# Output product of a hybrid backbone: 512 columns per product in four banks, gate rows fetched through DRAM, and tiles moved to other addresses modulo 128

## The chip, the cores and the metric

The kernel runs on one core of one Trainium2 chip, as one launch. The metric is the device time of that launch in microseconds, the median of several runs. TensorE (PE) multiplies, VectorE (DVE) and ScalarE (ACT) do elementwise work, GpSimd (POOL) does little here, and SyncE (SP) and ScalarE issue the DMA transfers.

## What is computed

A backbone of two layers over 1024 latent tokens and 256 context tokens, model width 1024, all float32. Each layer normalizes and modulates its input, projects it to 3840 columns, runs three branches (window attention, Conformer convolution, bidirectional gated recurrence, each 512 wide), and merges them:

```python
def merge_branches(h, ys, gs, w_branch, w_gate, b_gate, w_out):
    y = jnp.stack([yb.astype(h.dtype) * jax.nn.silu(gb) for yb, gb in zip(ys, gs)], axis=-2)
    proj = jnp.einsum('btnw,nwd->btnd', y, w_branch)
    g = jax.nn.sigmoid(h @ w_gate + b_gate).reshape(h.shape[:-1] + (N_BRANCH, D_MODEL))
    return jnp.sum(proj * g, axis=-2) @ w_out
...
        out = merge_branches(h, (y_att, y_conv, y_lru), (g_att, g_conv, g_lru),
                             w_branch[l], w_gate[l], b_gate[l], w_out[l])
        x_new = deepnorm_post(x, gate[:, None] * out, ln_g[l], ln_b[l])
```

The last product, `@ w_out`, is here called the output product; its result is scaled by `gate`, one value per output column, added to the residual and normalized. The context tokens take the same path in the first layer; in the last layer only what the latents read of them is computed.

## The kernel before

**Precision.** Every float32 operand of a large product is split into a high and a low float32r part (`whi`/`wlo` for weights, `hlhi`/`hllo` and `hchi`/`hclo` for latent and context activations, `yh`/`yl` for branch outputs). Each product is three matmuls, high by high, high by low, low by high, accumulated in one bank of PSUM. In the profile's rows a matmul stands as output <- moving operand, stationary operand, then the sizes of the stationary and the moving tile; each matmul has a weight load of its own (PEld).

**Phases.** Each layer has two phases. Phase 1 computes projections, branches and gate activations, in products whose moving operand is an activation tile of 512 latent tokens or 256 context tokens, and writes gate activations (`th_d`) and branch outputs (`y_d`) to DRAM. Phase 2 (`phase2`) runs over token groups: two groups of 512 latents, and in the first layer then one of 256 context tokens. For each group it does

- the branch products: 3 branches, 8 column chunks of 128, 4 blocks of 128 rows, 3 matmuls: 288 matmuls, moving `yh`/`yl` of 512 tokens, stationary the weights. DVE multiplies each result with a gate activation (`th`, a DMA of 256 KB for each chunk) and sums the three branches into `m`; ACT and DVE split the sum into `mg` (named `hlhi`, `hllo` in the rows, since it lies in the same buffers);
- `gate_rows`: the gate values, which lie along the partitions, are spread over rows of a 128 x 1024 tile `gt`: 8 float32 matmuls against the identity (16 records in the trace) and two copies from PSUM. This is done once for each set of gate values: for the latents in each layer, for the context in the first;
- the output product: for each quarter `qd` of the 1024 output columns (256 columns), for each tile `t` of 128 tokens, 24 matmuls with `mg` stationary and the weights moving, 256 columns each, into one bank; then two DVE operations on 256 columns (`tt` = product times gate row, `xp` = residual times alpha plus `tt`), and the first half of the statistics after the second quarter;
- in a second generator, `norm`: both layer norms of each finished token tile, and in the first layer transposes back (PE, 8 for each tile), modulation and splitting for the next layer.

**Order.** Work is cut into generators that a hand-written planner (`Driver`) interleaves by modelled costs, and the framework's scheduler then fixes each engine's order. Engines and DMA queues run their instructions in that order. Weights come in units of 512 KB (`Wt`): a DMA into `raw` (2 buffers), a copy to `whi` on ACT (4 buffers), a subtraction to `wlo` on DVE (4 buffers). `wfetch(2)` keeps two units ahead of the one in use.

**PSUM.** `psum()` gives one bank of 4 (tag `mm`), `psum2()` two banks together of 2 pairs. Phase 2 uses only `psum()`, for its products and for `norm`'s transposes.

**Addresses.** Tiles lie in SBUF at addresses that follow from the order in which pools are opened, from the left end and from the right end, and from the sizes of tiles (in bytes per partition). The first pool of constants begins at 4096 (scratch) + 128; the constants take 6688, the weights 40960, the activations `hT` 81920, the small tiles 2528. From these, the start addresses modulo 128:

| tiles | layer 0 | layer 1 |
|---|---|---|
| weights `whi`, `wlo`, `raw` | 32 | 32 |
| activations `hlhi`, `hllo`, `hchi`, `hclo`, and `mg` | 32 | 32 |
| branch outputs `yh`, `yl` in phase 2 | 0 | 96 |
| half tiles of phase 1 (`ph`, `qh`, gate weights `lwh`) | 96 | 0 |
| slots of 1328 floats (`vs`, `ks`, `xh`, `P`) | 0 and 64 in turn | 96 and 32 in turn |
| `csr` (4 columns for each of 8 blocks), `ident` | 0 | 0 |

All steps inside the large tiles are multiples of 128 bytes, so that a tile's start gives the residue of each of its blocks.

## Time and profile before

| | |
|---|---|
| median of 3 runs | 2345.81 us (2345.65 to 2347.58) |
| profiled execution, its own time | 2346.24 us |
| its span, first to last instruction | 2344.5 us |
| mean granted clock of TensorE | 0.992 of 2.4 GHz |

One execution is profiled, and rows come from it. A row of a group gives count, busy time, mean duration and the idle time before it. Matmuls overlap in the rows: the duration of one is longer than the step from its start to the next one's start, and the step is what a matmul costs when PE is never idle. Steps are therefore read from the starts in the timeline, over a run of matmuls without gaps.

### The profile page before, as it was taken

The page shows a single profiled execution, that of the slowest core. Times are in us where ns is not written, and L with a number is a line of the kernel's source. Part 1 is how long each engine was busy: PE and PEld are TensorE (multiplying, and loading weights), DVE is VectorE, ACT ScalarE, POOL GpSimd, SP SyncE. Part 2 cuts the span into 40 slices and gives each one's busy share as a digit, 9 for nine tenths or more (in the row PEclk, how much of TensorE's full clock was granted, in tenths as well). Part 3 has the DMA queues.
Part 4 walks back from the last instruction along what each step waited for, and adds up shares of the span by engine and source line. Part 5 has one row for each costly group of instructions (what it writes and reads, how often), then busy time and mean ns, then how long its engine had stood idle before and what let it go on. Part 6 is the DMA issues. An engine that isn't in the chain of part 4 may idle for free.

```text
span 2344.5 us, 32215 instructions
## 1 busy us (share of the span) xinstructions
PE 2280.8 (97%) x12253; PEld 1925.5 (82%) x12253; DVE 1750.5 (75%) x2588; ACT 1066.3 (45%) x1702; POOL 91.2 (4%) x136
## 2 busy tenths in 40 slices
PE   7999999999999999999998899999999999999998
PEld 3888888888888887888888878888888878778988
DVE  5679867869859875448888839979778887657776
ACT  4555553244444565323344535665344456543231
POOL 1000000000000111000101000000000011000000
PEclk8999999999999999999999999999999999999999
DMA  7222323433344332566565622223423334348482
GB/s 279 68 74 97 117 77 124 133 119 103 100 125 125 95 95 91 181 218 217 170 219 166 194 70 65 74 90 128 140 92 95 94 113 135 108 139 276 138 272 72
DMA packets 305819, 309.91 MB, mean 132 GB/s; under 512 B 20608, under 2 KB 239616, under 8 KB 305664
## 3 DMA queue, kind: packets, MB, share of 16 engines
q1 hardware_dynamic: 277152, 255.94, 34.5%
q10 hardware_dynamic: 28512, 51.92, 6.2%
q8 instruction: 96, 1.57, 0.3%
q14 instruction: 59, 0.48, 0.1%
HBM read 232.92 MB, written 74.87 MB: 131 GB/s over the span
## 4 chain that ended last, share of the span: by engine, by line
PE 88%; DVE 5%; ACT 3%; DMA 2%; issue 2%; SPq 0%; POOLq 0%; POOL 0%; ACTq 0%; DVEq 0%
PE ps L73 81%; PE yp L73 3%; PE pt L73 2%; PE pa L73 1%; DVE wlo L73 1%; DMA qd<-qd 1%; ACT whi L73 1%; DVE acc L73 1%; DVE P L73 1%; DVE pl L73 1%; DMA thl<-th 1%; DVE xp L73 0%; DMA raw<-in_w_ada_dram 0%; PE p L73 0%; ACT ph L73 0%
## 5 line engine op out<-in xcount | busy, mean ns | idle before, releaser
L73 PE MATMUL ps<-hlhi,whi 128*128 128x512 f32 x1728 | 683.1, 396 | 2.3 <-DVE gs L73 1.0
L73 PE MATMUL ps<-hllo,whi 128*128 128x512 f32 x1728 | 679.3, 393 | 0.0
L73 PE MATMUL ps<-hlhi,wlo 128*128 128x512 f32 x1728 | 677.7, 393 | 1.1 <-DVE wlo L73 1.1
L73 ACT ACTIVATE whi<-raw 128x1024 fp32r<-128x1024 f32 x240 | 253.8, 1058 | 440.6 <-PE ps L73 406.7
L73 DVE TENSOR_TENSOR wlo<-raw,whi 128x1024 fp32r<-128x1024 f32 x240 | 294.2, 1226 | 124.0 <-ACT whi L73 122.9
L73 PEld LDWEIGHTS ps<-hlhi,wlo 128*128 128x128 f32 x1728 | 325.7, 188 | 70.6 <-DVE wlo L73 2.0
L73 PEld LDWEIGHTS ps<-hlhi,whi 128*128 128x128 f32 x1728 | 326.3, 189 | 68.3 <-DVE pl L73 2.4
L73 PEld LDWEIGHTS ps<-hllo,whi 128*128 128x128 f32 x1728 | 326.1, 189 | 63.6 <-issue 0.7
L73 DVE SCALAR_TENSOR_TENSOR acc<-u,cwt,acc 128x1296 f32<-128x1296 f32 (+1 forms) x240 | 343.0, 1429 | 2.1
L73 PE MATMUL ps<-yh,whi 128*128 128x512 f32 (+1 forms) x480 | 178.0, 377 | 9.3 <-DVE thl L73 6.6
L73 PE MATMUL ps<-yl,whi 128*128 128x512 f32 (+1 forms) x480 | 178.2, 373 | 2.3 <-DVE yl L73 2.3
L73 PE MATMUL ps<-yh,wlo 128*128 128x512 f32 (+1 forms) x480 | 178.9, 374 | 0.0
L73 ACT ACTIVATE ph<-pt 128x512 fp32r<-128x512 f32 x160 | 93.8, 591 | 130.0 <-PE pt L73 124.5
L73 DVE TENSOR_TENSOR pl<-pt,ph 128x512 fp32r<-128x512 f32 x160 | 109.3, 687 | 50.7 <-ACT ph L73 49.3
L73 PE MATMUL ps<-whi,hlhi 128*128 128x256 f32 x512 | 144.3, 284 | 0.0
L73 PE MATMUL ps<-wlo,hlhi 128*128 128x256 f32 x512 | 144.0, 283 | 0.0
L73 PE MATMUL ps<-whi,hllo 128*128 128x256 f32 x512 | 142.6, 283 | 0.0
L73 ACT ACTIVATE P<-P,nm 128x640 f32<-128x640 f32 (+1 forms) x128 | 101.9, 797 | 82.1 <-DVE nm L73 82.1
L73 PE MATMUL ps<-hchi,whi 128*128 128x256 f32 x480 | 136.7, 285 | 2.1 <-ACT hchi L73 0.8
L73 PE MATMUL ps<-hchi,wlo 128*128 128x256 f32 x480 | 136.7, 285 | 0.9 <-DVE wlo L73 0.9
L73 PE MATMUL ps<-hclo,whi 128*128 128x256 f32 x480 | 135.9, 283 | 0.0
L73 DVE CUSTOM_DVE_ANT_0 P<-ps,m_mid,nsink 128x640 f32<-128x640 f32 (+1 forms) x112 | 93.3, 862 | 43.4 <-PE ps L73 42.0
(204 smaller groups left out, 3756.7 us busy)
## 6 DMA issues: line engine op xcount, KB each, us to landing
raw<-in_w_in_dram SPq DMA_DIRECT2D x60, 512.0 KB
raw<-in_w_branch_dram SPq DMA_DIRECT2D x60, 512.0 KB
raw<-in_w_ada_dram SPq DMA_DIRECT2D x48, 512.0 KB
raw<-in_w_gate_dram SPq DMA_DIRECT2D x48, 512.0 KB
th<-tg ACTq DMA_DIRECT2D x96, 256.0 KB
thl<-th SPq DMA_DIRECT2D x96, 256.0 KB
raw<-in_w_out_dram SPq DMA_DIRECT2D x40, 512.0 KB
yd<-gs ACTq DMA_DIRECT2D x48, 256.0 KB
```

Of the source, the lines that this page charges most:

```text
L73: return f(*a, **k)
```

## The change

Four edits.

1. The output product takes 512 output columns in a matmul. A unit of weights is 256 rows by 512 columns (still 512 KB). For each half `ch` of the columns and each unit `kp`, all token tiles of the group are multiplied, side by side in as many banks (two `psum2()` in the first half, four `psum()` in the second), and each is finished after the last unit. In the last group's second half four units are held and the tiles run one after the other. The two DVE operations work on 512 columns.
2. `gate_rows` transposes the 128 x 8 gate values once, copies 8 rows, writes them to DRAM and reads them back to all 128 partitions with a second DMA, both on SP's queue. It is done at the start of a group, ahead of the branch products, where it stood behind them.
3. Filler tiles of 96, 64, 64, 32 and 96 bytes (each set once by a memset on POOL), and slots of 1344 floats for 1328.
4. The scratch for dynamic DMAs is 1024 bytes for 4096.

```diff
--- before.py
+++ after.py
@@ -32 +32 @@
 
-SLOT = 1328
+SLOT = 1344
 NS, NHF, NW, NWL, NXP, NYY = 10, 14, 4, 2, 7, 6
...
@@ -206 +206 @@
 
+    def pad(pool_, n, tag):
+
+        if n:
+            pool.memset(pool_.tile([128, n // 4], F32, tag=tag, name=tag), 0.0)
+
+    pad(K, 96, "padk")
+    pad(H, 64, "padh1")
+    pad(SM, 32, "pads")
+    PR = ctx.enter_context(tc.tile_pool(name="padr", bufs=1, side="right"))
+    pad(PR, 96, "padr")
+
     def f32(ap):
...
@@ -239 +250 @@
     xs_d = DR.tile([T, D], F32, tag="xs", name="xs_d")
+    gate_d = [[DR.tile([D], F32, tag=f"gd{l}{s}", name=f"gd{l}{s}") for s in range(2)] for l in range(DEPTH)]
 
...
@@ -465 +477 @@
             hT[0, nt[0]] = alloc_h(nt[0], nt[2])
+            if nt is NT_C:
+                pad(H, 64, "padh2")
 
...
@@ -1111 +1125 @@
 
-    def gate_rows(l, s, dst):
-        for hf_ in range(2):
-            ps = psum()
-            for k in range(4):
-                kk = hf_ * 4 + k
-                pe.matmul(out=ps[:, k * 128:k * 128 + 128], lhsT=ada[l][:, 16 + kk, s:s + 1].to_broadcast([128, 128]),
-                          rhs=ident, start=True, stop=True)
-            dve.tensor_copy(dst[:, hf_ * 512:hf_ * 512 + 512], ps)
+    def gate_rows(l, s, dst, row):
+
+        ps = psum()
+        pe.transpose(ps[0:KD, 0:128], ada[l][:, 16:24, s], ident)
+        dve.tensor_copy(row[0:KD], ps[0:KD, 0:128])
+        sp.dma_start(out=gate_d[l][s].rearrange("(k p) -> k p", p=128), in_=row[0:KD])
+        sp.dma_start(out=dst, in_=gate_d[l][s].partition_broadcast(128))
 
...
@@ -1130 +1143 @@
         gt = RH.tile([128, D], F32, tag="gt", name="gt")
-        tt_first = [RH.tile([128, 256], F32, tag="tt", name="tt", bufs=2)]
+        tt_first = [RH.tile([128, 512], F32, tag="tt", name="tt", bufs=2)]
         m_first = [RH.tile([128, 2, 512], F32, tag="xp", name="m", bufs=NXP)]
...
@@ -1141 +1154 @@
                 for dp in range(4):
-                    units.append(w_branch[l, b][:, dp * 256:dp * 256 + 256])
-            for qd in range(4):
-                for kh in range(2):
-                    units.append(w_out[l][kh * 512:kh * 512 + 512, qd * 256:qd * 256 + 256])
+                    units.append((w_branch[l, b][:, dp * 256:dp * 256 + 256], 4, 256))
+            for ch in range(2):
+                for kp in range(4):
+                    units.append((w_out[l][kp * 256:kp * 256 + 256, ch * 512:ch * 512 + 512], 2, 512))
         wq, wi = [], [0]
...
             while len(wq) < n and wi[0] < len(units) and wlive[0] < NW:
-                wq.append(Wt(units[wi[0]].rearrange("(k p) n -> p k n", p=128), 4, 256))
+                src, a, b = units[wi[0]]
+                wq.append(Wt(src.rearrange("(k p) n -> p k n", p=128), a, b))
                 wi[0] += 1
...
@@ -1199 +1213 @@
                 ms, xp = [], []
+                if s != gs_:
+                    yield "pe"
+                    gt_, gs_ = gt_ if gs_ is None else RH.tile([128, D], F32, tag="gt", name="gt"), s
+                    gate_rows(l, s, gt_, RH.tile([128, 128], F32, tag="grow", name="grow"))
                 for bi_, b in enumerate(BR):
...
@@ -1246 +1264 @@
                             xq.give()
-                if s != gs_:
-                    yield "pe"
-                    gt_, gs_ = gt_ if gs_ is None else RH.tile([128, D], F32, tag="gt", name="gt"), s
-                    gate_rows(l, s, gt_)
                 for t in range(n // 128):
...
@@ -1262 +1276 @@
                 sts = []
-                for qds in ((0,), (1,), (2, 3)) if last and nt is groups[-1] else ((0,), (1,), (2,), (3,)):
-                    w2 = [wnext() for _ in range(2 * len(qds))]
-                    wfetch(2)
-                    for t, qd in [(t, qd) for t in range(n // 128) for qd in qds]:
-                        wa = w2[2 * (qd - qds[0]):2 * (qd - qds[0]) + 2]
-                        cq = slice(qd * 256, qd * 256 + 256)
-                        yield ("pe", wa[1].ready)
-                        ps = psum()
-                        i = 0
-                        for k in range(KD):
-                            for a, v in ((0, 0), (0, 1), (1, 0)):
-                                pe.matmul(out=ps[:, 0:256], lhsT=mg[a][:, k, t * 128:t * 128 + 128],
-                                          rhs=wa[k // 4][v][:, k % 4, :], start=(i == 0), stop=(i == 23))
-                                i += 1
-                            if k == 3:
-                                yield "pe"
-                        tt = tt_first.pop() if tt_first else RH.tile([128, 256], F32, tag="tt", name="tt", bufs=2)
-                        dve.tensor_tensor(out=tt, in0=ps[:, 0:256], in1=gt_[:, cq], op=ALU.mult)
-                        dve.scalar_tensor_tensor(out=xp[t][:, cq], in0=xp[t][:, cq], scalar=ALPHA, in1=tt, op0=ALU.mult,
-                                                 op1=ALU.add)
-                        if qd == 0:
-                            sts.append(SM.tile([128, 2, 6], F32, tag="st1", name="st1", bufs=8))
-                        if qd == 1:
-                            ln_half(xp[t], sts[t], 0)
-                        if qd == 3:
-                            fin.append((nt, t, xp[t], sts[t]))
-                    for w in w2:
+                nt_ = n // 128
+
+                def product(ps, t, kp, w):
+                    for k in range(2):
+                        for a, v in ((0, 0), (0, 1), (1, 0)):
+                            pe.matmul(out=ps, lhsT=mg[a][:, 2 * kp + k, t * 128:t * 128 + 128], rhs=w[v][:, k, :],
+                                      start=(kp == 0 and k == 0 and a == 0 and v == 0), stop=(kp == 3 and k == 1 and a == 1))
+
+                def finish(ps, t, ch):
+                    cq = slice(ch * 512, ch * 512 + 512)
+                    tt = tt_first.pop() if tt_first else RH.tile([128, 512], F32, tag="tt", name="tt", bufs=2)
+                    dve.tensor_tensor(out=tt, in0=ps, in1=gt_[:, cq], op=ALU.mult)
+                    dve.scalar_tensor_tensor(out=xp[t][:, cq], in0=xp[t][:, cq], scalar=ALPHA, in1=tt, op0=ALU.mult,
+                                             op1=ALU.add)
+                    if ch == 0:
+                        sts.append(SM.tile([128, 2, 6], F32, tag="st1", name="st1", bufs=8))
+                        ln_half(xp[t], sts[t], 0)
+                    else:
+                        fin.append((nt, t, xp[t], sts[t]))
+
+                for ch in range(2):
+                    if last and nt is groups[-1] and ch:
+                        w4 = [wnext() for _ in range(4)]
+                        for t in range(nt_):
+                            ps = psum()
+                            for kp, w in enumerate(w4):
+                                yield ("pe", w.ready)
+                                product(ps, t, kp, w)
+                            finish(ps, t, ch)
+                        for w in w4:
+                            w.free()
+                        continue
+                    if ch:
+                        pss = [psum() for _ in range(nt_)]
+                    else:
+                        two = [psum2() for _ in range(nt_ // 2)]
+                        pss = [two[t // 2][:, t % 2 * 512:t % 2 * 512 + 512] for t in range(nt_)]
+                    for kp in range(4):
+                        w = wnext()
+                        wfetch(2)
+                        for t in range(nt_):
+                            yield ("pe", w.ready)
+                            product(pss[t], t, kp, w)
+                            if kp == 3:
+                                finish(pss[t], t, ch)
                         w.free()
-                    if yq and len(nexty) < 4:
-                        yield "act"
-                        nexty.append(ysplit())
-                        yfetch()
+                        if kp % 2 and yq and len(nexty) < 4:
+                            yield "act"
+                            nexty.append(ysplit())
+                            yfetch()
                 if n > C:
...
@@ -1419 +1451 @@
 
-    nc = _bacc.Bacc("TRN2", target_bir_lowering=False, num_devices=1, dynamic_dma_scratch_size=4096)
+    nc = _bacc.Bacc("TRN2", target_bir_lowering=False, num_devices=1, dynamic_dma_scratch_size=1024)
     inputs = dict(inputs)
...
     arrays, args = {}, []
```

## Rows read from the trace of the kernel before

**Rows 1.** The page, busy time and share of the span, by engine.

```profile
PE 2280.8 (97%) x12253; PEld 1925.5 (82%) x12253; DVE 1750.5 (75%) x2588; ACT 1066.3 (45%) x1702; POOL 91.2 (4%) x136
```

**Rows 2.** Busy time of each engine by stretch, clock, DMA share and rate.

```profile
core 0: us, PE busy (x) PEld busy (x) DVE busy (x) ACT busy (x) POOL busy (x), PEclk, DMA share, GB/s
1026.00:1093.50 67.50, 67.50 (x291) 54.37 (x290) 47.12 (x65) 23.02 (x29) 0.00 (x0) 1.00 0.76 258
1141.30:1210.70 69.40, 69.40 (x311) 56.08 (x310) 63.87 (x102) 36.20 (x57) 6.76 (x7) 1.00 0.75 248
1258.10:1311.00 52.90, 40.99 (x314) 38.66 (x314) 48.32 (x97) 30.91 (x53) 7.80 (x8) 0.97 0.73 236
2108.40:2174.30 65.90, 65.90 (x289) 54.05 (x289) 47.90 (x66) 23.14 (x29) 0.00 (x0) 1.00 0.80 269
```

**Rows 3.** Groups of matmuls by tile and shape, PE.

```profile
L73 PE MATMUL ps<-whi,hlhi 128*128 128x256 f32 x512 | 144.3, 284 | 0.0
L73 PE MATMUL ps<-hchi,whi 128*128 128x256 f32 x480 | 136.7, 285 | 2.1 <-ACT hchi L73 0.8 <-ACT whi L73 0.7 <-DVE pl L73 0.4
L73 PE MATMUL yp<-ph,vs 128*128 128x512 f32 x160 | 67.9, 424 | 12.8 <-ACT ph L73 9.5 <-DVE pl L73 2.4 <-DVE yt L73 0.8
```

**Rows 4.** Timeline of PE around the first group's output product: start, us, work.

```profile
1093.31 0.40 PE L73 MATMUL ps<-yh,wlo 128*128 128x512 f32 x1
1093.54 1.95 PE L73 MATMUL ps<-ident,ada 128*128 128x128 f32 x16
1095.24 0.36 PE L73 MATMUL ps<-whi,hlhi 128*128 128x256 f32 x1
...
1141.27 0.28 PE L73 MATMUL ps<-whi,hllo 128*128 128x256 f32 x1
```

**Rows 5.** Timeline of PE, 24 context and 48 latent products of phase 1.

```profile
1012.56 0.28 PE L73 MATMUL ps<-hchi,whi 128*128 128x256 f32 x1
...
1015.31 0.28 PE L73 MATMUL ps<-hchi,wlo 128*128 128x256 f32 x1
1015.43 0.40 PE L73 MATMUL ps<-hlhi,whi 128*128 128x512 f32 x1
...
1026.11 0.39 PE L73 MATMUL ps<-hlhi,wlo 128*128 128x512 f32 x1
```

**Rows 6.** Timeline of PE, first and last of 288 branch products, three groups.

```profile
1026.34 0.40 PE L73 MATMUL ps<-yh,whi 128*128 128x512 f32 x1
...
2108.45 0.40 PE L73 MATMUL ps<-yh,whi 128*128 128x512 f32 x1
...
2174.16 0.40 PE L73 MATMUL ps<-yh,wlo 128*128 128x512 f32 x1
...
2222.26 0.40 PE L73 MATMUL ps<-yh,whi 128*128 128x512 f32 x1
...
2289.23 0.40 PE L73 MATMUL ps<-yh,wlo 128*128 128x512 f32 x1
```

**Rows 7.** Timeline of PE, matmuls of 256 columns at other distances.

```profile
147.44 0.28 PE L73 MATMUL ps<-whi,csr 128*4 128x256 f32 x1
...
148.37 0.39 PE L73 MATMUL ps<-hlhi,whi 128*128 128x512 f32 x1
...
1268.66 0.28 PE L73 MATMUL ps<-yl,whi 128*128 128x256 f32 x1
...
1269.25 0.28 PE L73 MATMUL ps<-yh,whi 128*128 128x256 f32 x1
```

**Rows 8.** Groups of DVE operations by shape.

```profile
L73 DVE TENSOR_TENSOR wlo<-raw,whi 128x1024 fp32r<-128x1024 f32 x240 | 294.2, 1226 | 124.0 <-ACT whi L73 122.9 <-PE pt L73 0.3
L73 DVE TENSOR_TENSOR tt<-ps,gt 128x256 f32<-128x256 f32 x72 | 30.0, 421 | 37.0 <-PE ps L73 36.9
L73 DVE TENSOR_TENSOR m<-m,thl 128x512 f32<-128x512 f32 x64 | 43.7, 689 | 0.7
```

**Rows 9.** SP's waits around the start of phase 2: total us, times, longest.

```profile
SPq L1170 <- DMA yd<-gs: 15.9, 2, 8.8
```

## The prediction, made before the change was run

> **What bounds the kernel now.** I read the page first: PE is busy for 2280.8 of 2344.5 us, 97%, DVE for 75% [rows 1]. Then the table by stretch: in phase 2 PE never rests over whole stages, 67.5 of 67.5 us and 69.4 of 69.4; only in the context group, 1258 to 1311, does it rest, for 11.9 us, while transfers run at 236 GB/s [rows 2]. So nearly everywhere a matmul costs its step from start to start, and removed steps come off the end time. The reader should take steps and not mean durations: a 256-column matmul lasts 284 ns in its group [rows 3] but the next starts after a far shorter time.
>
> Steps, as differences of starts divided by the number of steps between them:
>
> - output product, 256 columns, 384 matmuls: (1141.27 - 1095.24) / 383 = 120.2 ns [rows 4];
> - latent products of phase 1, 512 columns, 48 matmuls: (1026.11 - 1015.43) / 47 = 227.2 ns [rows 5];
> - context products of phase 1, 256 columns, 24 matmuls: (1015.31 - 1012.56) / 23 = 119.6 ns [rows 5];
> - branch products, 512 columns, 288 matmuls: (1093.31 - 1026.34) / 287 = 233.3 ns in layer 0; (2174.16 - 2108.45) / 287 = 229.0 ns and (2289.23 - 2222.26) / 287 = 233.3 ns in layer 1 [rows 4, 6].
>
> Two things stand in these numbers. In phase 1 the step grows by 227.2 - 119.6 = 107.6 ns for 256 more columns, 0.42 ns each, which is one cycle of the granted clock, 1.00 of 2.4 GHz in these stretches [rows 2]; so 12 to 13 ns of each matmul do not depend on its width, and two narrow ones pay them twice. And branch products have the shape of the latent products, yet take 2 to 6 ns longer. PE does not wait for anybody in either. What differs is where operands lie: by the address table, stationary and moving operand both start at 32 modulo 128 in the latent products (distance 0), while in the branch products `yh`/`yl` lie 32 away from the weights in layer 0 and 64 away in layer 1. That the distance is the cause is my inference.
>
> **The change, part by part.** The sum is made against the profiled execution's own 2346.2 us, 0.4 us over the median.
>
> *Width.* A pair of 256-column steps becomes one of 512: 2 x 120.2 - 227.2 = 13.2 ns, if stationary and moving stay at distance 0, which they do for latents (below). Four latent groups with 192 wide matmuls each are 768: 768 x 13.2 = 10.1 us. The context group has 96 wide ones, whose distance will be 64; I take the mean of the two steps seen there, 231.2: 96 x (240.4 - 231.2) = 0.9 us. All of it is on PE's path. The Trainium skill, "TensorE: Matmul & The Clock Gate", section "Back-to-back issue gap", gives N / 2.4 + 2.5 ns for a warm matmul; by it a pair would save 2.5 ns and the latents 1.9 us in place of 10.1. The rows, 120.2 and 227.2, do not agree with that page's extra of 2.5 ns, so the rows decide.
>
> *Gate rows.* 16 records hold PE from 1093.54 to 1095.24, 1.70 us [rows 4], three times: 5.1 us. One transpose of 128 columns is one such record, 1.70 / 16 = 0.11 us, so 4.8 us are gained. The new copy and two DMAs stand on DVE and on SP's queue; behind them on SP wait the transfers of weights, `th` and `y`. The result is needed some 70 us later, after the branch products, so its own latency is hidden; what the block on SP costs is a rival.
>
> *Addresses.* Constants now start at 1024 + 128 = 9 x 128 and take 6688 + 96 = 53 x 128; so weights lie at 0. In `hT` a filler of 64 puts the context tiles at 64, and the next filler puts the latent tiles and `mg` at 0. Small tiles take 2528 + 32 = 20 x 128, and a right-hand filler of 96 takes the other end from 96 to 0; slots take 5376 = 42 x 128. So all large tiles but the context's lie at 0. Three results follow.
>
> First, branch products of latents go to distance 0, at 227.2: 576 x 6.1 in layer 0, 288 x 1.8 and 288 x 6.1 in layer 1, together 3.5 + 0.5 + 1.8 = 5.8 us. Second, 1440 context products of phase 1 (three groups of 480 [rows 3]) go from distance 0 to 64. No row shows full 128-column weights at 64 with 256 columns. The nearest: with `csr`, whose distances vary, (148.37 - 147.44) / 8 = 116 ns, and branch products of the context at 32, (1269.25 - 1268.66) / 5 = 118 ns [rows 7]. Both are below 119.6, unlike what 512 columns do. I take 117.1: 1440 x 2.5 = 3.6 us. Ends: 116, 5 us gained; or 2 ns lost as at 512 columns in the better case, 2.9 us lost. Third, the attention's value products (320 of 512 columns, half of them in [rows 3]) go to distance 0, at most 320 x 6.1 ns = 2.0 us. Part of it goes under the waits seen in that group, and the score products change their distances too; I take 0.5 us, with ends 0 and 2.0. Products of latents in phase 1 keep distance 0.
>
> The page of the skill just named says, in "Step-by-step: what each phase is for", that the two operands have independent SBUF read ports and that loading weights takes no bandwidth from the running matmul. By it no distance matters and these 9.9 us, with a little of the context's output product, are not gained; the 227.2 and 233.3 speak against it. This is a rival below.
>
> *Finishing.* 72 pairs of 421 ns become 36 pairs of about 689 ns [rows 8], 11 us less for DVE in all, off the path except at the end: after the last matmul the two operations are 2 x 0.27 = 0.5 us longer. They now come in bursts: at the end of a first half four tiles need 4 x 3 x 0.69 = 8.3 us while PE takes 4 x 6 x 0.227 = 5.4 us. The other four banks cover this, since PE goes on in them with weights that were split before. The cover is gone in the last group's second half: its third and fourth unit are fetched at the end of the first half, and their `wlo` can stand behind the burst on DVE. The burst starts 1.4 us into that 5.4 us and so ends 4.3 us after it; one `wlo` of 1.23 us [rows 8] makes 5.5 us, and the first two units give PE only 2 x 6 x 0.227 = 2.7 us to do. Bounds 0 and 2.8, taken as 1.5 us, since the scheduler may set the order otherwise.
>
> *Context group.* There transfers and PE share the bound. Its part of the gains above is 1.6 + 0.9 us; half is taken back, 1.3 us. Weight units have rows of 2 KB for 1 KB in the output product, which I count as nothing. The memsets of the fillers are five short operations on an engine that is busy for 4%, and the scratch is used by no transfer here: nothing at either end, but for well under 1 us if PE's first matmul should wait for them.
>
> Sum: 10.1 + 0.9 + 4.8 + 5.8 + 3.6 + 0.5 = 25.7 gained, 0.5 + 1.5 + 1.3 = 3.3 lost, 22.4 us net. On the scale of the median, 2345.8 - 22.4 = 2323.4 us.
>
> **Rivals.**
>
> A. *Distance modulo 128 does nothing.* Then width and gate rows alone count: 10.1 + 1.3 + 4.8 - 3.3 = 12.9, 2332.9 us. For it: layer 1 shows 229.0 and 233.3 at one and the same distance, so something else acts too. Against it: three of three stretches at other distances are slower than 227.2. Chance 0.12.
>
> B. *Another bound takes over in the branch stages.* DVE is busy for 63.9 of 69.4 us in the second group of layer 0, and the stages move 248 to 269 GB/s [rows 2]. If either holds PE at the old pace, the 5.8 us go: 2329.2 us. Against it: PE ran the fastest of the three stretches at the highest rate, 269 GB/s. Chance 0.15.
>
> C. *Banks.* In the second half of a group all four `mm` banks are held for 96 x 0.227 = 21.8 us, and `norm`'s transposes need one. If they are pushed behind the product, `norm` of two token tiles moves past it and half of that time comes back at the layer boundary: some 11 us, 2335 us. Against it: the context stage that follows has 11.9 us of rest. Chance 0.06.
>
> D. *Slower: SP's queue stops at the gate rows.* The write must wait for DVE's copy, the read for the write's landing; meanwhile no `th` is issued. One wait on a landing of a like write took 8.8 us [rows 9]; twice that is 17.6 us. Three `th` buffers cover three chunks of 12 matmuls, 8.4 us. Uncovered 9.2 us, three times, 27.6 us: 2351 us. It makes the kernel slower by over 0.2% only if each stop lasts over 17.4 us. Against it: the copy waits for one PE transpose at a stage where DVE works for 47 of 67 us. Chance 0.04.
>
> **How the numbers follow.** The forecast, 2318 to 2329 us by its own bounds, has 0.60; 0.03 is left for what I do not see. 8 times in 10 the time should lie in 2314 to 2335 us, which takes in A and B. 0.2% is 4.7 us, about what a measurement of this kernel can tell: faster means below 2341.1. The forecast, A, B and C lie there, 0.93, of which I take off 0.01 for a C of twice its price. That 0.01 and 0.02 of the unseen make no change, D and the other 0.01 make it slower: 0.92 faster, 0.03 the same, 0.05 slower.
>
> **What would show it.** In the profile after: output product at about 227 ns from start to start, a group in 43.6 us for 46.1; branch products at 227 in all three latent groups and both layers; context products of phase 1 under 119.6; no gap of 1.7 us between branch and output product. A would show branch products still at 233 with PE never at rest; B new PE waits for `thl` or weights inside them; C transposes bunched after a product; D long waits of SP at the gate rows' DMAs and PE waiting for `thl` just after a group's start. I am wrong above all if context products become slower at distance 64, or if new waits in the output product exceed 3 us.

## The result and the profile after

The changed kernel takes 2376.89 us (median of 4 runs, 2375.86 to 2379.18), the kernel before 2345.85: a ratio of 1.0132 with a 95% interval of 1.0114 to 1.015. It is 31 us slower, where the prediction had it 22 us faster. The profiled execution took 2377.07 us, its span is 2375.3.

The page of the kernel after, busy time by engine, to set against [rows 1]:

```profile
PE 2292.4 (97%) x11344; PEld 1879.2 (79%) x11344; DVE 1734.1 (73%) x2513; ACT 1067.5 (45%) x1702; POOL 90.0 (4%) x141
```

PE has 909 instructions fewer and is busy 11.6 us longer. The table by stretch, for stages that answer to [rows 2] (a branch stage with its neighbours, the context group, the first branch stage of layer 1):

```profile
core 0: us, PE busy (x) PEld busy (x) DVE busy (x) ACT busy (x) POOL busy (x), PEclk, DMA share, GB/s
1146.90:1220.30 73.40, 71.36 (x318) 57.53 (x317) 69.14 (x115) 36.41 (x58) 9.45 (x8) 1.00 0.71 233
1264.60:1320.00 55.40, 37.66 (x272) 36.36 (x270) 48.56 (x96) 26.59 (x44) 9.04 (x9) 0.85 0.64 209
2133.10:2199.90 66.80, 66.80 (x290) 54.10 (x289) 48.25 (x68) 22.95 (x29) 0.00 (x0) 1.00 0.82 271
```

Branch stages still keep PE busy, but for 2.0 us of the first one shown; the context group has lost PE time and clock. The timeline of PE after, for the places of [rows 4, 5, 6]: 24 context and 48 latent products of phase 1, the branch products of the first group, its output product.

```profile
1021.23 0.28 PE L73 MATMUL ps<-hchi,whi 128*128 128x256 f32 x1
...
1023.94 0.28 PE L73 MATMUL ps<-hchi,wlo 128*128 128x256 f32 x1
1024.06 0.39 PE L73 MATMUL ps<-hlhi,whi 128*128 128x512 f32 x1
...
1034.99 0.40 PE L73 MATMUL ps<-hlhi,wlo 128*128 128x512 f32 x1
...
1035.25 0.48 PE L73 MATMUL ps<-yh,whi 128*128 128x512 f32 x1
...
1102.03 0.40 PE L73 MATMUL ps<-yh,wlo 128*128 128x512 f32 x1
1102.26 0.40 PE L73 MATMUL ps<-whi,hlhi 128*128 128x512 f32 x1
...
1146.83 0.39 PE L73 MATMUL ps<-whi,hllo 128*128 128x512 f32 x1
```

Context products take (1023.94 - 1021.23) / 23 = 117.8 ns, latent products (1034.99 - 1024.06) / 47 = 232.6, branch products (1102.03 - 1035.25) / 287 = 232.7, the output product (1146.83 - 1102.26) / 191 = 233.4. Only the first is as predicted. The latent products were at 227.2 [rows 5] and were not meant to change at all.

All of PE's steps, from one start to the next, summed by kind over both traces (a wait counts with the instruction ahead of it):

| kind (instructions before) | before, us | after, us | difference |
|---|---|---|---|
| latent products of phase 1 (5184) | 1206.6 | 1231.0 | +24.4 |
| branch products of the context (288) | 45.8 | 57.0 | +11.2 |
| from the last matmul's start to the end | 9.04 | 18.46 | +9.42 |
| branch products of latents (1152) | 268.0 | 270.8 | +2.8 |
| output product, latents (1536) | 184.5 | 179.3 | -5.2 |
| gate matmuls | 5.1 | 0.1 | -5.0 |
| `norm`'s and other transposes | 16.4 | 11.8 | -4.6 |
| context products of phase 1 (1440) | 177.5 | 175.3 | -2.2 |
| output product, context (192) | 23.1 | 22.6 | -0.5 |

The sum is 30.3 us; the spans differ by 30.8.

### The profile page after: what moved, and what is told of

Read it like the earlier page. It is cut to its first block, busy times and chain, and to the rows that moved or that the text cites. A ratio compares the mean times of both kernels' runs of the same rounds, so it can differ in the third digit from the quotient of the medians.

```text
span 2375.3 us, 30308 instructions
## 1 busy us (share of the span) xinstructions
PE 2292.4 (97%) x11344; PEld 1879.2 (79%) x11344; DVE 1734.1 (73%) x2513; ACT 1067.5 (45%) x1702; POOL 90.0 (4%) x141
## 4 chain that ended last, share of the span: by engine, by line
PE 88%; DVE 5%; ACT 3%; DMA 2%; issue 1%; POOL 0%; SPq 0%; DVEq 0%; ACTq 0%; POOLq 0%
PE ps L73 81%; PE yp L73 3%; PE pt L73 2%; PE pa L73 1%; DVE wlo L73 1%; ACT whi L73 1%; DVE xp L73 1%; DVE P L73 1%; DMA raw<-in_w_ada_dram 0%; DVE pl L73 0%; DMA thl<-th 0%; DVE acc L73 0%; ACT hf L73 0%; PE p L73 0%; DMA qd<-qd 0%
## 5 line engine op out<-in xcount | busy, mean ns | idle before, releaser
L73 PE MATMUL ps<-hlhi,wlo 128*128 128x512 f32 x1728 | 684.6, 397 | 1.1 <-DVE wlo L73 1.1
L73 PEld LDWEIGHTS ps<-yh,whi 128*128 128x128 f32 x480 | 91.8, 192 | 22.3 <-DVE thl L73 4.2
L73 ACT ACTIVATE tg<-ps,drv 128x512 f32<-128x512 f32 (+1 forms) x120 | 76.6, 638 | 65.9 <-PE ps L73 65.4
L73 PEld LDWEIGHTS ps<-yl,whi 128*128 128x128 f32 x480 | 92.1, 192 | 16.9
```

What stands on the lines that cost most here:

```text
L73: return f(*a, **k)
```

## The experiments

Distances below are start of the stationary tile minus start of the moving rows, modulo 512 bytes. Before: latent and context products and the output product 0, branch products of latents 32 in layer 0 and 192 in layer 1. After: latent products 384, output product 128 (64 for the context), branch products 384, context products 448. Modulo 128 those of after are 0, but for the context's 64 and 448, which are 64, as the prediction had them.

### First: which property of the addresses

Three theories. The first: distance modulo 512 (or 256) sets the step, not modulo 128. The second: the start itself modulo 128 does. The third: the order of the work does.

**Fillers enlarged to a distance of 0 modulo 512**, from the changed kernel:

```diff
-    pad(PR, 96, "padr")
+    pad(PR, 224, "padr")
...
-                pad(H, 64, "padh2")
+                pad(H, 448, "padh2")
```

> The changed kernel with larger fillers (448 for 64 bytes behind the context tiles, 224 for 96 at the right end), so that the latent tiles and the branch outputs start at a multiple of 512 bytes from the weights, where they start 128 past such a multiple in the changed kernel. All start residues modulo 128 stay as in the changed kernel. Theory 1 (the step of a 512-column matmul hangs on the distance of its two operands modulo 512, at least modulo 256): latent products go from 232.6 to about 228.5 ns a step, output and branch products from 233 to 227, some 5184 x 4 + 1920 x 6 ns = 32 us less PE time, 2345 us. Theory 2 (it hangs on the start residue modulo 128 itself, 32 being better than 0): no change, 2377 us. Theory 3 (the order of the work and its waits took the time, and steps do not hang on addresses): 2377 us.

Measured: 2347.73 us, ratio to before 0.9994 [0.9981, 1.0008]. PE's timeline, the first group's branch products and output product:

```profile
1026.42 0.48 PE L73 MATMUL ps<-yh,whi 128*128 128x512 f32 x1
...
1091.60 0.39 PE L73 MATMUL ps<-yh,wlo 128*128 128x512 f32 x1
1091.82 0.39 PE L73 MATMUL ps<-whi,hlhi 128*128 128x512 f32 x1
...
1135.12 0.39 PE L73 MATMUL ps<-whi,hllo 128*128 128x512 f32 x1
```

(1091.60 - 1026.42) / 287 = 227.1 ns and (1135.12 - 1091.82) / 191 = 226.7: the predicted steps, in both products. Two larger fillers give back 29 of the 31 us.

**All tiles 32 bytes further on, distances as in the changed kernel:**

```diff
-    pad(K, 96, "padk")
+    pad(K, 128, "padk")
...
-    pad(PR, 96, "padr")
+    pad(PR, 64, "padr")
```

> The changed kernel with all large tiles moved 32 bytes on (fillers of 128 for 96 at the left, 64 for 96 at the right), all distances between tiles as in the changed kernel. Theory 1 (distance modulo 512): latent products stay at 232.6 ns, 2377 us. Theory 2 (start residue modulo 128): latent products fall to 228.5, output and branch products to 227, some 2345 us. Theory 3: 2377 us.

Measured: 2379.99 us, 1.013 [1.011, 1.0151]; latent products 232.5 ns, output product 233.3. The start itself does not matter here; the second theory falls.

**The kernel before, with 128 bytes ahead of the latent tiles:**

```diff
             hT[0, nt[0]] = alloc_h(nt[0], nt[2])
+            if nt is NT_C:
+                pool.memset(H.tile([128, 32], F32, tag="padh2", name="padh2"), 0.0)
```

> The kernel before with one filler of 128 bytes between the context tiles and the latent tiles, so that latent tiles keep their residue modulo 128 but stand 128 past a multiple of 512 from the weights. Theory 1: latent products of phase 1 rise from 228.5 to about 232.5 ns a step, some 20 us, 2366 us. Theory 2 and theory 3: unchanged, 2346 us.

Measured: 2365.75 us, 1.007 [1.0046, 1.0095]. Its 48 latent products, from PE's timeline:

```profile
1024.32 0.39 PE L73 MATMUL ps<-hlhi,whi 128*128 128x512 f32 x1
...
1035.25 0.39 PE L73 MATMUL ps<-hlhi,wlo 128*128 128x512 f32 x1
```

(1035.25 - 1024.32) / 47 = 232.6 ns. Order and instructions are those of before; one 128-byte tile makes the latent products as slow as in the changed kernel. The third theory falls.

**The changed kernel without its address edits** (no fillers, slots and scratch as before):

> The changed kernel without its edits of addresses (no fillers, slots of 1328, scratch of 4096): the wide output product and the gate rows by way of DRAM alone. Theories 1 and 2: latent products at 228.5 ns as before, output product at 227; what is left of the loss are waits, at the end (9.5 us) and in the context group (11 us), against 15 us less PE work: about 2350 us. Theory 3: 2377 us.

Measured: 2356.7 us, 1.0029 [1.0016, 1.0041]: some 7 us more than expected, so width and gate rows alone lose some 7 us against before (by the ratio). Latent products are at 228.7 ns (mean over all steps without a wait, as in before) and the output product at 227.0; what is lost is the tail and the context group, below.

**The step by itself.** A kernel that does nothing but stream products, 96 (`NMM`) in a row for each distance `dist`, with `st` and `mv` a multiple of 512 bytes apart; `base` is 0, or 8 elements for starts 32 bytes further on:

```python
        o = dist // 4
        for i in range(NMM):
            m = i % 4 * 1024 + base
            s = i % 3 * 512 + base + o
            pe.matmul(out=ps[:, 0:width], lhsT=st[:, s:s + 128], rhs=mv[:, m:m + width], start=(i == 0), stop=(i == NMM - 1))
```

> Nothing of the reference is computed (x is copied to the output). TensorE alone streams 96 products in a row for each of 18 distances, from the start of the moving rows to the start of the stationary tile modulo 512 bytes, in steps of 16 or 32 bytes, for 512 and for 256 columns, each twice, and for four distances a third time with both tiles 32 bytes further on. Theory that the distance alone sets the step, with nothing else on the chip at work: 512 columns take about 226.8 ns at distance 0, 232 to 233 ns at 64 and 128, 230 ns at 256; 256 columns take 120 ns at 0, 113.4 ns at 64, 117.4 ns at 448; the third time repeats the first two within 1 ns. Rival, that the differences come from the traffic beside the products (the other engines, DMA, which buffer is being filled): all distances take the same time within 1 ns.

PE's timeline. The name of an output tile spells the width (`wf` 512, `wt` 256 columns) and the distance in letters for digits (a is 0, so `age` is 064); a `b` ahead marks starts 32 bytes further on. The difference of two starts, over 96, is the step.

```profile
67.14 21.92 PE L57 MATMUL wfaaax<-mv,st 128*128 128x512 f32 x96
88.90 21.93 PE L57 MATMUL wfabgx<-mv,st 128*128 128x512 f32 x96
...
155.45 22.55 PE L57 MATMUL wfagex<-mv,st 128*128 128x512 f32 x96
177.85 22.65 PE L57 MATMUL wfajgx<-mv,st 128*128 128x512 f32 x96
200.33 22.47 PE L57 MATMUL wfbcix<-mv,st 128*128 128x512 f32 x96
222.65 22.57 PE L57 MATMUL wfbgax<-mv,st 128*128 128x512 f32 x96
...
867.98 11.67 PE L57 MATMUL wtaaax<-mv,st 128*128 128x256 f32 x96
879.49 11.53 PE L57 MATMUL wtabgx<-mv,st 128*128 128x256 f32 x96
...
913.51 11.05 PE L57 MATMUL wtagex<-mv,st 128*128 128x256 f32 x96
924.40 11.69 PE L57 MATMUL wtajgx<-mv,st 128*128 128x256 f32 x96
...
1376.94 11.47 PE L57 MATMUL bwtagex<-mv,st 128*128 128x256 f32 x96
1388.25 11.57 PE L57 MATMUL bwtbcix<-mv,st 128*128 128x256 f32 x96
```

With 512 columns: (88.90 - 67.14) / 96 = 226.7 ns at 0, 233.3 at 64, (222.65 - 200.33) / 96 = 232.5 at 128. With 256: 119.9 at 0, (924.40 - 913.51) / 96 = 113.4 at 64, but (1388.25 - 1376.94) / 96 = 117.8 at the same 64 with both starts 32 bytes on. The whole map, at distances in bytes, in which the second pass repeats the first within 0.1 ns:

| columns | step, ns, at distances |
|---|---|
| 512 | 226.7 at 0, 16, 256; 229.0 at 192, 448; 232.4 at 128, 384; 233.3 at 32, 48, 64, 160, 224, 288, 320, 416, 480; 234.2 to 234.3 at 96, 352 |
| 256 | 113.3 at 64; 117.3 to 117.8 at 48, 192, 224, 320, 352, 448, 480; 118.3 to 118.7 at 16, 32, 128, 288; 119.9 to 120.0 at 0, 96, 160, 256, 384, 416 |

With no other engine at work beside the products, the distance makes the differences that the kernel showed, and the rival is out. For 512 columns the map repeats after 256 bytes, not after 128: distance 256 took 226.7 ns, where the theory had 230. In one place the theory fails: of the eight products tried again 32 bytes further on, seven came within 1 ns of the first time, but 256 columns at 64 took 117.8 ns for 113.3. There the distance does not settle the step.

### Second: the tail, the context group, the gate rows

All of these have weights and latents at a distance of 0 modulo 512, so that the address loss is out of the way.

**Single banks in the last group** (its halves trade: four single banks in the first, then the first bank of a pair for each tile in the second):

```diff
-                            ps = psum()
+                            ps = psum2()[:, 0:512]
...
-                    if ch:
+                    if ch or last and nt is groups[-1]:
                         pss = [psum() for _ in range(nt_)]
```

> The changed kernel with the fillers enlarged so that weights and latents lie a multiple of 512 bytes apart (as in the run before this one that measured 2347.7 us), and in the last group of four tiles of each layer the output tiles take single banks again instead of pairs of banks in one tile, in the order in which each becomes free. Theory that the longer tail (18.6 us after the last product, 9.1 before the change) comes from the pairing, which keeps the four tiles' finishing work together at the end: the tail falls to about 9 to 10 us and the time to about 2339 us. Rival, that the tail comes from the order in which the four tiles share each weight unit, whatever their banks: the tail stays near 18 us and the time at 2347 to 2348 us.

Measured: 2339.02 us, 0.9958 [0.9943, 0.9974]. In the changed kernel, ACT's timeline holds the reason; the bracket gives the idle time before and what ended it:

```profile
2329.30 1.06 ACT L73 ACTIVATE whi<-raw 128x1024 fp32r<-128x1024 f32 x1 [4.54 <-PE ps L73]
2345.82 1.06 ACT L73 ACTIVATE whi<-raw 128x1024 fp32r<-128x1024 f32 x1 [15.46 <-PE ps L73]
```

The last unit of weights waits 15.46 us for the buffer of the first half's last unit. In PE's order the products of that unit into the second bank of each pair stand between products of the second half, behind DVE's read of the first bank. So all four tiles wait for the last unit and finish together: DVE's first reads of the four results (`tt`) start between 2353.75 and 2358.16. PE's last matmul starts at 2356.82, and DVE then has half of the finishing and both passes of all norms still to do:

```profile
2358.16 0.67 DVE L73 TENSOR_TENSOR tt<-ps,gt 128x512 f32<-128x512 f32 x1
...
2359.41 1.27 DVE L73 SCALAR_TENSOR_TENSOR xp<-xp,mv,lng 128x1024 f32<-128x1024 f32 x1
...
2368.77 2.47 DVE L73 SCALAR_TENSOR_TENSOR xp<-xp,rs,lnb 128x1024 f32<-128x1024 f32 x2
```

With single banks the last unit of weights waits 4.33 us, the tiles follow one another (`tt` at 2313.30, 2314.66, 2321.42 and 2326.16), and the end of the run is

```profile
2325.12 0.39 PE L73 MATMUL ps<-whi,hllo 128*128 128x512 f32 x1
...
2326.16 0.68 DVE L73 TENSOR_TENSOR tt<-ps,gt 128x512 f32<-128x512 f32 x1
...
2331.43 1.28 DVE L73 SCALAR_TENSOR_TENSOR xp<-xp,rs,lnb 128x1024 f32<-128x1024 f32 x1 [0.44 <-POOL rs L414]
```

The span is 2336.6, so the tail is 11.5 us for 18.5. The theory holds, with 7 of the 9 us; where the other 2.5 come from was not tried.

**Gate rows on PE again, at their old place, wide product kept:**

> The changed kernel with weights and latents a multiple of 512 bytes apart, and the gate rows spread by TensorE with ones as before the change, at their old place, instead of by way of DRAM. Theory that the wait of 11.9 us of TensorE after the context products of layer 0 comes from the finishing work of four tiles on VectorE: the wait stays at about 12 us, and the time rises by the gate products' 5 us to about 2352 us. Rival, that it comes from the gate rows' way through the SP queue: the wait goes, and the time falls by about 7 us to 2341 us.

Measured: 2346.11 us, 0.9994 [0.9981, 1.0008]. PE's longest wait in the context stage is still there:

```profile
PE ps L73 <- ACT xp L73: 10.6, 1, 10.6
```

The rival falls: the gate rows do not cause it. Nor did their matmuls cost the 5 us that theory added: the time is 1.6 us less than with the rows by way of DRAM, a difference that the intervals do not tell from none.

**The old output product, with gate rows by way of DRAM:**

> The output product as before the change (256 columns, one tile after the other), with the gate rows by way of DRAM and weights and latents a multiple of 512 bytes apart. Theory that the group of four tiles causes both the wait of 11.9 us and the longer tail: both go, the output products take 120 ns a piece of 256 columns again (about 5 us more in the sum than 512 columns at 227 ns), and the time is about 2333 us. Rival, that both come from the gate rows or the addresses: they stay, and the time is about 2352 us.

Measured: 2339.24 us, 0.996 [0.9945, 0.9975]. The wait on `xp` is gone from the context stage; the longest is now

```profile
PE ps L73 <- DVE thl L73: 4.6, 4, 2.5
```

and the tail is 8.9 us. Both belong to the four tiles side by side. The time is 6 us over what was expected; the next run, which lacks only the gate rows by way of DRAM, puts that on them: they gave nothing.

**The kernel before with the addresses alone:**

> The kernel before the change with the addresses alone: branch weights, output weights and latents all a multiple of 512 bytes apart. Theory that the distance modulo 512 sets the step: the branch products go from 232.3 to 227 ns (1152 of them, minus 6 us), the context products of phase 1 from 119.3 to 117.4 ns (1440, minus 3 us), the latent products stay at 228.6, and the time is 2336 to 2338 us. Rival, that the addresses pay only together with the wide product: no change, 2346 us.

Measured: 2335.18 us, 0.9948 [0.9929, 0.9966]. Branch products fall from 268.0 to 261.8 us in all. It is faster than both kernels, and it lies 4 us under the same kernel with gate rows by way of DRAM; the intervals of the two overlap.

**Eight shared buffers for seven**, from the single-bank version (`NXP` 8):

> The changed kernel with weights and latents a multiple of 512 bytes apart and single banks in the last group (2339.0 us), with eight instead of seven buffers that merged sums and rows of x share. Theory that TensorE's wait of 11.6 us in the context products of layer 0 is one for a buffer: four token tiles that finish together hold four of seven, the context group takes three, and its fourth waits until the first tile has been normalised and transposed; with eight the wait falls below 4 us and the time to 2328 to 2332 us. Rival, that the wait is VectorE's pile of finishing work, whatever the buffers: transposes wait as long wherever they stand, 2337 to 2340 us.

Measured: 2341.71 us, 0.9967 [0.9955, 0.998]. The wait on `xp` shrinks and others take its place:

```profile
PE ps L73 <- ACT xp L73: 6.3, 1, 6.3
PE ps L73 <- DVE thl L73: 3.2, 3, 1.5
PE ps L73 <- DVE yl L73: 2.0, 2, 1.1
```

The branch products of the context still sum to 53.4 us, 54.3 with seven buffers. A free buffer takes 5 us from this one wait, but none of the time that the theory promised comes back, and it falls.

**No pairs of banks in the other groups either:**

```diff
-                        two = [psum2() for _ in range(nt_ // 2)]
-                        pss = [two[t // 2][:, t % 2 * 512:t % 2 * 512 + 512] for t in range(nt_)]
+                        pss = [psum2()[:, 0:512] if t % 2 else psum() for t in range(nt_)]
```

> The changed kernel with weights and latents a multiple of 512 bytes apart and single banks in the last group (2339.0 us), and in all other groups too no pair of banks in one tile: two tiles of tokens take banks of their own of the one kind, two the first bank of a pair each. Theory that the pairs delay the context stage as they delayed the tail, by holding back products into the second bank of a pair: TensorE's wait of 11.6 us after the first context products falls below 5 us, and the time to 2328 to 2333 us. Rival, that four tiles which finish at one time pile their work on VectorE whatever banks they lie in: the wait stays at 10 to 12 us and the time at 2336 to 2340 us.

Measured: 2337.73 us, 0.9957 [0.9943, 0.9971]; the wait is 9.3 us. VectorE's timeline at its end:

```profile
1262.05 1.27 DVE L73 SCALAR_TENSOR_TENSOR xp<-xp,mv,lng 128x1024 f32<-128x1024 f32 x1
1263.76 0.16 DVE L73 SCALAR_TENSOR_TENSOR nb<-mv,rs 128x1 f32<-128x1 f32 x1 [0.44 <-POOL rs L414]
1264.28 1.28 DVE L73 SCALAR_TENSOR_TENSOR xp<-xp,rs,lnb 128x1024 f32<-128x1024 f32 x1 [0.36 <-POOL rs L414]
```

From 1252 to 1264 VectorE rests for only these 0.44 and 0.36 us: finishing and norms of four tiles, merges and `wlo` stand there one behind the other, while PE waits. The pairs are not the cause, though the wait came out a little below the rival's 10 us. That four tiles finish at one time is what the remaining runs agree on; a version in which they finish one by one in this group alone was not run, so the share of VectorE's order in it stays open.

### Third: versions that use the map

**Merged rows 64 bytes on, old product of 256 columns** (on the kernel with the addresses alone; tiles grow by 512 bytes, and the merged rows start 16 elements in):

```diff
-    def alloc_h(ti, n):
+    def alloc_h(ti, n, merged=False):
...
+        o = 16 if merged and n == 512 else 0
+        ts = [H.tile([128, KD * n + 128], F32R, tag=tg, name=f"{tg}{v}", bufs=b) for v in ("hi", "lo")]
+        return tuple(t[:, o:o + KD * n].rearrange("p (k n) -> p k n", k=KD) for t in ts)
```

> The kernel before the change with weights and latents a multiple of 512 bytes apart (2335.2 us), and in addition the merged rows of the latent groups, the stationary operand of the output product, moved 64 bytes on inside their tiles; the product keeps its 256 columns. Theory of the map by distance (256 columns: 120.0 ns at 0, 113.3 ns at 64): 1536 output products take 113.4 ns instead of 120.0, minus 10 us, 2325 us. Rival, that 256 columns are dearer than half of 512 in this kernel whatever the addresses: 120 ns and 2335 us.

Measured: 2330.08 us, 0.9911 [0.9897, 0.9925]. The output product falls from 184.6 to 176.6 us, not to 174.2: of its seven stretches without a pause five take 113.3 ns a product and two 117.8.

**Context rows too:**

```diff
-        o = 16 if merged and n == 512 else 0
+        o = (16 if n == 512 else 32) if merged else 0
...
-    pad(H, 64, "padh1")
+    pad(H, 448, "padh1")
...
-                pad(H, 448, "padh2")
+                pad(H, 64, "padh2")
```

> As the run before, with the context rows of phase 1 also placed so that the weights lie 64 bytes past them (they lay 448 past, 117.4 ns a piece); the moving rows then start 192 bytes past a multiple of 512 instead of 256. Theory that for 256 columns the distance alone decides: 1440 context products at 113.4 ns instead of 117.4, minus 6 us, 2319 us. Rival, that the start of the moving rows counts too (in the map 64 bytes of distance took 113.3 ns at one start and 117.8 ns 32 bytes further on): 117 to 118 ns, and no change, 2325 us.

Measured: 2325.29 us, 0.9901 [0.9888, 0.9915], the fastest of all, 23 us under the kernel before on the same chip (2348.33). The output product of layer 1's first group, 384 products of 256 columns, from PE's timeline:

```profile
2159.79 0.37 PE L73 MATMUL ps<-whi,hlhi 128*128 128x256 f32 x1
...
2203.30 0.28 PE L73 MATMUL ps<-whi,hllo 128*128 128x256 f32 x1
```

(2203.30 - 2159.79) / 383 = 113.6 ns: two narrow products cost what one wide one costs, without four banks. Context products of phase 1, though, took 116.7 ns in the mean: of their 48 stretches of 12 or more without a pause, 16 lie between 113.5 and 114.8 and nearly all others near 117.7. The rival's number is nearer than the theory's, and the step over the run before is within the intervals. Its cause, the start of the moving rows, is not shown by this: in the run before, all latent output products have the same starts modulo 512 by the program's addresses, 256 for the moving weights and 320 for the merged rows, and still took 113.3 ns in five stretches and 117.8 in two.

## Why the prediction was wrong

The step that failed is in the paragraph on addresses: "Products of latents in phase 1 keep distance 0." They kept distance 0 modulo 128, which is what the prediction counted; modulo 512 they went from 0 to 384, because the two fillers of 64 bytes in `hT` add 128 to a distance that had been a multiple of 512. 5184 products at 232.6 for 228.6 ns (means over all steps without a wait) are 20 of the 24.4 us; the waits between them grew by 3 us more. Rows 5 gave one good distance and rows 6 two others; nothing in them said after how many bytes the rule repeats, and 128 was taken from the residues that the change itself speaks of. For the context products a loss was among the bounds; for the latent products there was none, and this one unpriced sentence carried 1206.6 us, half of PE's time. From 22.4 us gained to 30.8 lost is 53 us; the three kinds of products whose distance came out wrong make 38 of them (latent products 24.4, branch products of latents 8.6, output product 4.9), the tail 7.4 and the context group 5.3.

Point by point, by the prediction's own terms:

- **Width, 10.1 us.** The mechanism is right at distance 0: at 226.7 ns the wide product sums to 174.3 us, 10.2 below the 184.5 of before. At 233.4 it gave 5.2. But width is not the only way to these 10 us: at distance 64 two narrow products take 2 x 113.3 ns.
- **Context's output product, 0.9 us.** It gave 0.5; the step at 64 is 233.2, not the mean 231.2.
- **Gate rows, 4.8 us.** PE lost 5.0 us of them and the end did not come sooner: 2339.2 us with the rows by way of DRAM against 2335.2 without in the old product, 2347.7 against 2346.1 in the wide one. With the old product PE instead waits 5.1 us for `whi` at the start of layer 1, 0.4 with the gate rows on PE; that the queue is the reason was not tried by itself. SP's waits for the landing of the gate rows' writes were 6.6 us in three, in the changed kernel.
- **Branch products, 5.8 us.** They lost 2.8 at distance 384 and gained 6.2 at 0 modulo 512. Size right, place wrong.
- **Context products of phase 1, 3.6 us.** 2.2; the step went to 117.4 in the mean for 117.1 assumed.
- **Finishing at the end, 0.5 + 1.5 us.** 9.4. The prediction saw the last units of weights come late behind DVE. What it missed is that pairs of banks hold back the products that free the buffer, so that four tiles' norms come after the last matmul.
- **Context group, 1.3 us.** Its branch products' steps grew by 11.2 us, while the transposes' shrank by 4.6. After PE's wait of 11.9 us its granted clock also falls, to 0.85 in the mean of the stretch from 1264.6 to 1320:

```profile
1285.45 0.90 PE L73 MATMUL ps<-ident,xp 128*128 128x128 f32 x3 [11.94 <-ACT xp L73]
...
1287.43 0.41 PE L73 MATMUL ps<-yl,whi 128*128 128x256 f32 x1
1287.64 0.41 PE L73 MATMUL ps<-yh,wlo 128*128 128x256 f32 x1
```

Steps are 0.21 us there for 0.12, until about 1291.3: the lower of its two levels, 1.2 GHz for 2.4.

Of the rivals, A is out: distance does act, and by more than was priced, though not modulo 128. B did not happen: branch products reach 227 ns once the distance is right. C had the right place, transposes ahead of PE's context products, and its price of 11 us was near the 11.9, but by luck: the transposes wait for `xp`, not for a bank. D's stops were shorter than its price, 6.6 us in three waits for a landing where it took 8.8 for one; what the gate rows lost instead stands above. The page that the prediction weighed, the Trainium skill, "TensorE: Matmul & The Clock Gate", section "Step-by-step: what each phase is for", lets a weight load run beside a matmul without taking from its reads; the map, 226.7 to 234.3 ns for one shape with nothing else at work, does not agree, and the measurement decides. The gap of N / 2.4 + 2.5 ns that the prediction set against its rows is given on that page of the Trainium skill, in "Back-to-back issue gap", for an isolated matmul and not for a stream with weight loads, so the rows were not a test of it.

## What to carry to other kernels

An edit that moves tiles must be priced over every product that reads them, not over those it is meant for; a term "stays as it is" needs a bound like any other. A rule found at two or three addresses has a period that they do not show: stream the shape by itself over all distances first, one short run. And work that finishes in parallel on the fast engine arrives as one pile on the next one: look at what stands behind it there, at the end of the kernel above all.

## What the runs showed of the hardware

- The step of a float32r product with its own weight load depends on the distance between the two operands in SBUF: 226.7 to 234.3 ns for 512 columns, with a period of 256 bytes over the distances tried; 113.3 to 120.0 for 256 columns, where distance 0, the best for 512, is among the worst, and where 256 bytes are no period (113.3 at 64, 117.8 at 320).
- Some distances have two steps. For 256 columns at 64 they are 113.3 and 117.8 ns, kept over up to 384 products in a row and changed, in the stretches read, only where PE paused or did other work between; the map shows one at one start and the other 32 bytes further on, the run with merged rows both at the same starts modulo 512. Branch products at distance 192 took 229.0 and 233.3 in the two groups of layer 1 before [rows 6], and 228.9 in both groups in the run without fillers; the map has 229.0. This is the difference "at one and the same distance" that spoke for rival A. What picks between the two was not found.
